# A two-layer RWKV-7 and latent-attention trunk: token lerps as a scaled sum on ScalarE and VectorE instead of GpSimd differences, and a new order at the start

## The chip, the core and the metric

The kernel runs on one core of one Trainium2 chip. The metric is device time in microseconds for one execution. The core has TensorE (PE: matmul, with its weight loads shown apart as PEld), VectorE (DVE), ScalarE (ACT), GpSimd (POOL) and SyncE (SP), which here only issues transfers. Each engine takes its instructions in the order of its own queue and waits at semaphores for the others.

## What is computed

The input, 512 tokens of width 1024 with 16 learned tokens put ahead of them (528 in all), goes through two layers. The first is an RWKV-7 mixer, the second a latent attention; the changed code is at the start of the first:

```python
h = concatenate([meta, x])
u = rms_norm(h, norm_pre[0])
u_prev = pad(u, one row ahead)[:-1]
dx = u_prev - u
# for each of six weights c = r, k, v, g, w_lo, a_lo, with a vector mu_c of 1024 numbers
h_c = (u + mu_c * dx) @ W_c
w = -softplus(-(w0 + tanh(w_lo) @ w2)) - 0.5
a = sigmoid(a0 + a_lo @ a2)
# then a recurrence over the tokens for 32 heads, its output normed, times silu(g), times W_out
```

Here `u + mu_c * dx` is the "lerp" of a token and the one before it.

## The kernel before

**Layout.** A token tile is [128 channels x 528 tokens], so the 1024 channels are 8 tiles, k = 0 to 7. The tile of the normed token has one column more, a zero ahead: columns 1 to 528 are u, columns 0 to 527 are the token before. To keep float32 precision at the speed of a faster form, each operand of a big product is split in a rounded high part and a rest, and three products are summed (high by high, high by rest, rest by high). So each token tile is split by ScalarE (a copy, the high part) and VectorE (a difference, the rest), and each 128x512 piece of weights by ScalarE (copy) and GpSimd (difference).

**Stages of the first layer.** `norm` reads the 8 tiles, squares them on ScalarE, sums them over the channels (on TensorE, by a product with a matrix of ones), and makes u. `lerps` runs in two lanes (even and odd k), each with one buffer (`sq` or `inv`) for the lerp; it takes the six weights in the order c = 2 (v), 4, 5 (the two small ones, "lora"), 3 (g, stored in DRAM), 1 (k), 0 (r). So there are 48 lerps, 8 for each c. `gemm` makes the projections, 48 matmuls each: v0 to v2 together, then v3, v4, lora 4, v5, lora 5, v6 to v13, k0, r0, k1, r1, v14, v15, k2, r2 and so on, and last 16 of g. `decays` makes w and a for all 16 head pairs (128 matmuls) when the lerps are done. `prepare`, `within`, `sides`, `invert`, `recur` and `finish` do the recurrence pair by pair; `prepare` begins behind the last of the decays. The projections of later pairs and of g fill TensorE meanwhile, and what is left of them runs behind the last pair.

**What sets the order.** All stages are generators that yield small steps. `Flow.run` picks among them the one that could start first, by a table of costs, and so writes out the queue of every engine beforehand; on the chip only the semaphores count. `flow.warm` names an f16 product into an unused part of a PSUM bank, which `Flow.cold` puts in where TensorE would idle, as a fill. The event "norm" is raised when the norm's factor (`ysq`) is made. `yield flow.until("norm")` so moves a step back in the written order; it is no wait on the chip.

**Names in the trace.** Tiles are reused, so the names say little at the start: u for k = 0 to 7 lies in SV, KBt, MR, KB, ALR, ALR, ALR, vx; the raw tokens, and then dx, lie beside them (the last in M). The split lerps of c = 2 lie in the other halves of SV, KBt, MR and so on; those of the others in `x`, and in `k` and `r` for c = 3. `w` is a split weight, `wraw` (or `X`) the raw one. All recorded instructions have one line, L322 (L327 after the change), that of the recorder.

Of the kernel before, what the change touches and what calls it, by code (L numbers as in the profile page):

```python
# [5 lines left out]
F32 = mybir.dt.float32  # L6
F32R = mybir.dt.float32r
F16 = mybir.dt.float16
AF = mybir.ActivationFunctionType
ALU = mybir.AluOpType  # L10
# [4 lines left out]
T = 528  # L15
# [46 lines left out]
class K:  # L62
# [14 lines left out]
    def consts(self):  # L77
        nc = self.nc
        cp = self.cp = self.pool("consts", 1)
        self.par = cp.tile([128, Par.n], F32, name="par")  # L80
        self.ones, self.ident, self.center = (cp.tile([128, 128], F32, name=n) for n in ("ones", "ident", "center"))
        self.bones = cp.tile([128, 128], F32, name="bones")
        self.omka = cp.tile([128, NP], F32, name="omka")
        nc.gpsimd.memset(self.ones, 1.0)
        scalars = cp.tile([128, 3], F32, name="scalars")
        for i, (name, x) in enumerate((("eps_gn", GN_EPS), ("one", 1.0), ("eps_rms", RMS_EPS))):
            t = scalars[:, i : i + 1]
            setattr(self, name, t)
            nc.gpsimd.memset(t, x)

    def load(self, nc):

        nc.sync.dma_start(self.par, self.a["par"])
        yield
        nc.sync.dma_start(self.ident, self.a["cst"][:, 0:128])
        yield
        nc.sync.dma_start(self.center, self.a["cst"][:, 128:256])
        yield
        o, w = Par.off["k_a"]
        nc.vector.tensor_scalar(self.omka, self.par[:, o : o + w], -1.0, 1.0, ALU.mult, ALU.add)  # L100
        nc.vector.tensor_copy(self.bones, self.center)
        nc.vector.scalar_tensor_tensor(self.center, self.center, -1.0 / 64, self.ident, ALU.mult, ALU.add)
        yield
# [354 lines left out]
class Layer0:  # L458
# [19 lines left out]
    def tl(self, bufs, shape, tag, dt=F32):  # L478
        return self.l[bufs].tile(list(shape), dt, name=self.g.nm(tag), tag=tag)
# [26 lines left out]
    def tables(self):  # L506

        nc = self.nc
        yield self.flow.until("x")
        yield from self.g.load(nc)  # L510
        for i in range(2):
            raw = self.tl(1, (128, 320), ("Mb", "Qb")[i])
            nc.sync.dma_start(raw, self.g.a["cst"][:, 256 + 320 * i : 576 + 320 * i])
            yield
            nc.vector.tensor_copy(self.masks[:, 5 * i : 5 * i + 5], raw.rearrange("p (m t) -> p m t", t=64))
            yield
        m = self.masks.rearrange("p m t -> p (m t)")

        self.bank, self.outs = self.psum("pc", 512, 1), self.psum("py", 512, 1)
        self.flow.cut[self.bank.tensor.name] = 128  # L520
        self.flow.cut[self.outs.tensor.name] = 256
        self.flow.warm = self.bank[:, 256:512], m[:, 0:128], m[:, 128:384]

    def norm(self):

# [6 lines left out]
        for k in range(KT):  # L532
# [4 lines left out]
            if k == KT - 1:  # L537
                nc.event("x")
            yield
        self.dx = xs  # L540
        self.place()
        part = [tl(1, (128, T), "P"), tl(1, (128, T), "gx")]
        nc.scalar.preload_act_table_set(EXP_LN)
        for k in range(KT):
            if k < 2:
                nc.scalar.activation(part[k], xs[k], AF.Square)
            else:
                sq = tl(1, (128, T), ("c", "a")[k % 2])
                nc.scalar.activation(sq, xs[k], AF.Square)
                yield  # L550
                (nc.gpsimd if k in (3, 5) else nc.vector).tensor_tensor(part[k % 2], part[k % 2], sq, ALU.add)
            yield
        out = self.two()
        for i in range(2):
            for (q, v), (b, e) in zip(out, HALVES):
                nc.tensor.matmul(v, g.ones, part[i][:, b:e], start=(i == 0), stop=(i == 1))
            yield
        rstd = tl(1, (128, T), "ysq")
        for (q, v), (b, e) in zip(out, HALVES):
# [4 lines left out]
        nc.event("norm")  # L564
        for k in range(KT):
            u = self.u[k]
            nc.vector.scalar_tensor_tensor(u[:, 1:], self.dx[k], g.p("norm_pre0", k), rstd, ALU.mult, ALU.mult)
            yield
            nc.gpsimd.tensor_tensor(self.dx[k], u[:, :T], u[:, 1:], ALU.subtract)
            nc.event(("u", k))  # L570
            yield
        self.places += [self.spare, tl(1, (128, T), "ysq", F32R)]
# [14 lines left out]
    def lerps(self, lane):  # L587
# [5 lines left out]
        for c in (2, 4, 5, 3, 1, 0):  # L593
            if c in late:
                yield self.flow.until(late[c])
            for k in range(lane, KT, 2):
                yield self.flow.until("u" if k == KT - 1 else ("u", k))
                xc = tl(1, (128, T), ("sq", "inv")[lane])
                nc.vector.scalar_tensor_tensor(xc, self.dx[k], g.p(f"mu{c}", k), self.u[k][:, 1:], ALU.mult, ALU.add)
                yield  # L600
                if c == 3:
                    h, l = tl(2, (128, T), "k", F32R), tl(2, (128, T), "r", F32R)
# [118 lines left out]
    def decays(self, lane):  # L721
# [9 lines left out]
        def read(j):  # L731
            t = tl(1, (128, 256), names[0])
            nc.sync.dma_start(t, g.a["w2a2"][j])
            return t

        raw = read(lane)
        yield flow.until(("lora", 4), ("lora", 5), ("lerps", 0), ("lerps", 1))
        for j in range(lane, NP, 2):
# [525 lines left out]
    def stages(self):  # L1264
        self.later = []
        self.x = {c: {} for c in range(6)}
        self.units()
        return [self.finish(), self.recur(1), self.recur(0), self.sides(), self.invert(0), self.invert(1), self.within(), self.prepare(), self.tables(), self.norm(),
                self.lerps(0), self.lerps(1), self.decays(0), self.decays(1)], [self.gate(), self.regate(), self.reload()]


WRAW = 2
# [928 lines left out]
```

## Time and profile before

| | us |
|---|---|
| median of 3 runs | 1610.45 |
| lowest and highest | 1608.45, 1613.81 |
| the profiled execution, its own time | 1609.79 |
| its span in the trace | 1608.0 |
| TensorE busy | 1463.8 |
| VectorE busy | 1034.9 |
| ScalarE busy | 942.4 |
| GpSimd busy | 733.9 |

The profiled execution lies 0.66 us below the median. 1.8 us of its time lie outside the span of the trace. A busy time of TensorE holds the latency of its products, which overlap, so a busy engine is not one at its peak.

### The profile page before, as it was taken

To read this page: it belongs to the slowest core of one execution; us is meant where nothing else is said; L and a number is where in the kernel's file an instruction comes from. 1 tells how busy PE (TensorE), PEld (TensorE's weight loads), DVE (VectorE), ACT (ScalarE), POOL (GpSimd) and SP (SyncE) were. 2 spreads that over 40 slices of the span, in tenths; PEclk is the share of its full clock that TensorE was granted. 3 is DMA by queue.
4 is the path that set the end of the run, shared out by engine and by line. 5 is a ranking of instruction groups with operands and counts; after the bars stand their busy time and mean duration, and the time that the engine had idled before them with its cause. 6 is when DMAs were issued, how large, how long until landed. Compare 5 with 4: busy or idle time off the path is not lost. (4 is left out here: it accounts for less than half of the span.)

```text
span 1608.0 us, 33360 instructions
## 1 busy us (share of the span) xinstructions
PE 1463.8 (91%) x12404; PEld 1301.2 (81%) x12404; DVE 1034.9 (64%) x2304; ACT 942.4 (59%) x2467; POOL 733.9 (46%) x877
## 2 busy tenths in 40 slices
PE   3899988899998998999998999999999999989997
PEld 3898877888887887888887899998778778877786
DVE  7995688787788877778777333035476666656503
ACT  3556655767766667677777674445555545544532
POOL 4453555444544435444445565745523222322654
PEclk7999999999999999999999999999999999999998
DMA  3456622122122122112422257533211111211332
GB/s 113 133 188 223 205 81 74 43 68 68 55 64 66 61 68 68 49 61 88 143 74 82 69 164 253 171 101 93 82 46 48 53 46 54 53 51 45 112 94 84
DMA packets 84690, 148.49 MB, mean 92 GB/s; under 512 B 9392, under 2 KB 18480, under 8 KB 84528
## 3 DMA queue, kind: packets, MB, share of 16 engines
q1 hardware_dynamic: 84528, 146.37, 28.9%
q8 instruction: 97, 1.59, 0.4%
q14 instruction: 65, 0.53, 0.1%
HBM read 112.87 MB, written 33.46 MB: 91 GB/s over the span
## 5 line engine op out<-in xcount | busy, mean ns | idle before, releaser
L322 POOL TENSOR_TENSOR w<-wraw,w 128x512 fp32r<-128x512 f32 (+1 forms) x278 | 371.6, 1343 | 478.8 <-ACT w L322 448.6
L322 PE MATMUL pg<-x,w 128*128 128x264 f32 x2064 | 337.5, 299 | 7.7 <-ACT k L322 3.2
L322 PEld LDWEIGHTS pg<-x,w 128*128 128x128 f32 x2064 | 272.7, 189 | 13.7 <-ACT k L322 5.7
L322 ACT ACTIVATE w<-wraw 128x512 fp32r<-128x512 f32 (+1 forms) x278 | 170.2, 615 | 135.7 <-DMA wraw<-wo 58.5
L322 POOL COPY Sd<-SV 64x64 f32<-64x64 f32 x256 | 73.1, 286 | 187.9 <-DVE SV L322 180.3
L322 PE MATMUL pb<-u,w 128*128 128x512 f32 x384 | 106.2, 405 | 11.9 <-DVE sg L322 11.9
L322 PE MATMUL pg<-lat,w 128*128 128x512 f32 (+1 forms) x480 | 108.5, 367 | 4.9 <-DVE q L322 3.1
L322 PEld LDWEIGHTS pg<-lat,w 128*128 128x128 f32 x480 | 80.6, 197 | 17.4 <-DVE q L322 3.5
L322 PEld LDWEIGHTS pb<-u,w 128*128 128x128 f32 x384 | 68.4, 190 | 25.8 <-DVE sg L322 14.2
L322 PE MATMUL pg<-O,w 128*128 128x512 f32 x336 | 79.1, 395 | 3.2 <-ACT acc L322 1.5
L322 PEld LDWEIGHTS pg<-O,w 128*128 128x128 f32 x336 | 62.9, 188 | 19.1 <-ACT acc L322 1.9
L322 DVE SCALAR_TENSOR_TENSOR SV<-Sd,PC,pc 64x64 f32<-64x64 f32 x224 | 59.8, 279 | 22.3 <-PE pc L322 17.5
L322 PE MATMUL pc<-xs,Qd 128*128 128x64 f32 x288 | 54.4, 286 | 20.4 <-ACT xs L322 19.0
L322 PEld LDWEIGHTS <-Mb 128*128 128x128 f16 x1152 | 59.0, 98 | 16.4 <-issue 6.4
L322 POOL TENSOR_TENSOR Lb<-M,Mh 64x256 f16<-64x256 f32 (+1 forms) x64 | 50.4, 787 | 42.8 <-ACT Mh L322 38.8
L322 PEld LDWEIGHTS pc<-xs,Qd 128*128 128x128 f32 x288 | 41.4, 189 | 34.3 <-ACT xs L322 29.8
L322 PE MATMUL pc<-SV,KBt 128*128 128x128 f32 x256 | 54.2, 312 | 9.5 <-DVE SV L322 7.6
L322 DVE SCALAR_TENSOR_TENSOR sg<-sg,par,rs 128x264 f32<-128x264 f32 x32 | 16.0, 532 | 71.9 <-ACT rs L322 71.9
L322 DVE TENSOR_TENSOR Xs<-pw,masks 128x128 f16<-128x128 f32 (+1 forms) x160 | 47.7, 301 | 21.4 <-PE pw L322 9.6
L322 DVE COPY SV<-pc 64x64 f32<-64x64 f32 x176 | 36.3, 225 | 38.4 <-ACT SV L322 32.7
L322 PE MATMUL pw<-Tm,Mb 128*128 128x32 f16 (+1 forms) x864 | 54.7, 180 | 4.8 <-ACT Tm L322 3.8
L322 PE MATMUL pc<-SV,ALR 128*128 128x128 f32 x288 | 57.2, 286 | 1.1 <-ACT xs L322 0.5
(375 smaller groups left out, 3906.7 us busy)
## 6 DMA issues: line engine op xcount, KB each, us to landing
wraw<-wr SPq DMA_DIRECT2D x120, 256.0 KB, 2.9
wraw<-wo SPq DMA_DIRECT2D x64, 256.0 KB, 2.7
wraw<-wi SPq DMA_DIRECT2D x46, 256.0 KB, 2.7
d_v<-gx SPq DMA_DIRECT2D x16, 264.0 KB, 3.0
d_c<-o SPq DMA_DIRECT2D x16, 264.0 KB, 2.4
c<-d_c SPq DMA_DIRECT2D x16, 264.0 KB, 3.0
a<-d_a SPq DMA_DIRECT2D x16, 264.0 KB, 3.1
vx<-d_v SPq DMA_DIRECT2D x16, 264.0 KB, 2.9
```

What stands on the lines that cost most here:

```text
L322: getattr(eng, method)(*args, **kw)
```

## The change

Six edits, all at the start of the first layer:

1. GpSimd's eight differences `dx = u_prev - u` are gone. A lerp was one VectorE instruction, `mu * dx + u`. It is now one ScalarE instruction, `(1 - mu) * u` (a copy with a scale for each channel, from the new small table `ommu`), and one VectorE instruction, `mu * u_prev +` that. Both write the lane's one buffer.
2. The norm's squares have a tile each and are summed by pairs (four VectorE sums, where there were four on VectorE and two on GpSimd), and each pair is multiplied by the ones on TensorE (eight products of 264 columns, where there were four).
3. `flow.warm` is set before anything is loaded, on the matrix of ones read as f16, instead of behind the load of the masks. Fill can stand from the first us.
4. The loads of `ident`, `center` and the masks, and the first of `w2a2`, are written behind the event "norm"; those of weights come ahead of them.
5. `omka`, `bones` and `center` move with their loads.
6. In the list of stages the lerps stand ahead of `norm`, so that they win where two steps could start at about the same time.

```diff
--- before.py
+++ after.py
+        self.ommu = cp.tile([128, 6 * KT], F32, name="ommu")
...
-    def load(self, nc):
+    def load(self, nc, flow):
 
         nc.sync.dma_start(self.par, self.a["par"])
         yield
+        o = Par.off["mu0"][0]
+        nc.vector.tensor_scalar(self.ommu, self.par[:, o : o + 6 * KT], -1.0, 1.0, ALU.mult, ALU.add)
+        yield
+        yield flow.until("norm")
         nc.sync.dma_start(self.ident, self.a["cst"][:, 0:128])
...
     def tables(self):
 
         nc = self.nc
+
+        self.bank, self.outs = self.psum("pc", 512, 1), self.psum("py", 512, 1)
+        self.flow.cut[self.bank.tensor.name] = 128
+        self.flow.cut[self.outs.tensor.name] = 256
+        c = self.g.ones.bitcast(F16)
+        self.flow.warm = self.bank[:, 256:512], c[:, 0:128], c
         yield self.flow.until("x")
-        yield from self.g.load(nc)
+        yield from self.g.load(nc, self.flow)
...
-        self.flow.warm = self.bank[:, 256:512], m[:, 0:128], m[:, 128:384]
...
-        part = [tl(1, (128, T), "P"), tl(1, (128, T), "gx")]
         nc.scalar.preload_act_table_set(EXP_LN)
-        for k in range(KT):
-            if k < 2:
-                nc.scalar.activation(part[k], xs[k], AF.Square)
-            else:
-                sq = tl(1, (128, T), ("c", "a")[k % 2])
-                nc.scalar.activation(sq, xs[k], AF.Square)
+        out = self.two()
+        for i, tags in enumerate((("P", "gx"), ("c", "a"), ("sq", "inv"), ("k", "r"))):
+            part = [tl(2 if i == 3 else 1, (128, T), t) for t in tags]
+            for k in range(2):
+                nc.scalar.activation(part[k], xs[2 * i + k], AF.Square)
                 yield
-                (nc.gpsimd if k in (3, 5) else nc.vector).tensor_tensor(part[k % 2], part[k % 2], sq, ALU.add)
-            yield
-        out = self.two()
-        for i in range(2):
+            nc.vector.tensor_tensor(part[0], part[0], part[1], ALU.add)
+            yield
             for (q, v), (b, e) in zip(out, HALVES):
-                nc.tensor.matmul(v, g.ones, part[i][:, b:e], start=(i == 0), stop=(i == 1))
+                nc.tensor.matmul(v, g.ones, part[0][:, b:e], start=(i == 0), stop=(i == 3))
             yield
...
-            nc.gpsimd.tensor_tensor(self.dx[k], u[:, :T], u[:, 1:], ALU.subtract)
             nc.event(("u", k))
...
                 xc = tl(1, (128, T), ("sq", "inv")[lane])
-                nc.vector.scalar_tensor_tensor(xc, self.dx[k], g.p(f"mu{c}", k), self.u[k][:, 1:], ALU.mult, ALU.add)
+                n = KT * c + k
+                nc.scalar.activation(xc, self.u[k][:, 1:], AF.Copy, scale=g.ommu[:, n : n + 1])
+                yield
+                nc.vector.scalar_tensor_tensor(xc, self.u[k][:, :T], g.p(f"mu{c}", k), xc, ALU.mult, ALU.add)
                 yield
...
+        yield flow.until("norm")
         raw = read(lane)
...
-        return [..., self.prepare(), self.tables(), self.norm(),
-                self.lerps(0), self.lerps(1), self.decays(0), self.decays(1)], [...]
+        return [..., self.prepare(), self.tables(), self.lerps(0), self.lerps(1), self.norm(),
+                self.decays(0), self.decays(1)], [...]
```

Three places show how the written order moves.

VectorE's queue, from the first normed token on, before (SV, KBt, MR, KB, ALR with `par` and `ysq` are the norm's; `sq` and `inv` the lerps; SV_275 the rest of the first split):

```order
L322 SCALAR_TENSOR_TENSOR SV_246<-SV_246,par,ysq_337 128x528
L322 SCALAR_TENSOR_TENSOR KBt_247<-KBt_247,par,ysq_337 128x528
L322 SCALAR_TENSOR_TENSOR MR_248<-MR_248,par,ysq_337 128x528
L322 SCALAR_TENSOR_TENSOR sq_359<-SV_246,par 128x528
L322 SCALAR_TENSOR_TENSOR KB_249<-KB_249,par,ysq_337 128x528
L322 SCALAR_TENSOR_TENSOR ALR_250<-ALR_250,par,ysq_337 128x528
L322 TENSOR_TENSOR SV_275<-sq_359,SV_275 128x528
L322 SCALAR_TENSOR_TENSOR ALR_250<-ALR_251,par,ysq_337 128x528
L322 SCALAR_TENSOR_TENSOR sq_371<-MR_248,par 128x528
L322 SCALAR_TENSOR_TENSOR inv_362<-KBt_247,par 128x528
```

The same place after the change:

```order
L327 SCALAR_TENSOR_TENSOR SV_249<-SV_249,par,ysq_346 128x528
L327 SCALAR_TENSOR_TENSOR KBt_250<-KBt_250,par,ysq_346 128x528
L327 SCALAR_TENSOR_TENSOR MR_251<-MR_251,par,ysq_346 128x528
L327 COPY bones<-center 128x128
L327 SCALAR_TENSOR_TENSOR center<-center,ident 128x128
L327 SCALAR_TENSOR_TENSOR sq_364<-SV_249,par,sq_364 128x528
L327 SCALAR_TENSOR_TENSOR inv_370<-KBt_250,par,inv_370 128x528
L327 SCALAR_TENSOR_TENSOR KB_252<-KB_252,par,ysq_346 128x528
L327 CAST masks<-Mb_376 128x320
L327 CAST masks<-Qb_384 128x320
L327 TENSOR_TENSOR SV_290<-sq_364,SV_290 128x528
L327 TENSOR_TENSOR KBt_291<-inv_370,KBt_291 128x528
```

Before, the constants' work stood ahead of the first normed token, and the rest of the first lerp came behind five of the norm's instructions. Now `bones` and `center` and the masks' two casts stand among the first lerps, two lerps go side by side, and the first rest comes behind four of the norm's.

ScalarE's queue where the lerps of c = 4 begin, before (`x` is the high part of a lerp, `w` that of a weight, `gx` the copy of a projection):

```order
L322 ACTIVATE x_497<-inv_488 128x528
L322 ACTIVATE w_513<-X_183_353 128x512
L322 ACTIVATE x_520<-sq_508 128x528
L322 ACTIVATE x_550<-sq_542 128x528
L322 ACTIVATE x_559<-inv_532 128x528
L322 ACTIVATE x_578<-sq_569 128x528
L322 ACTIVATE x_593<-inv_587 128x528
L322 ACTIVATE w_610<-wraw_500 128x512
L322 ACTIVATE x_613<-sq_602 128x528
```

And after, at the same lerps:

```order
L327 ACTIVATE sq_508<-SV_249,ommu 128x528
L327 ACTIVATE inv_520<-KBt_250,ommu 128x528
L327 ACTIVATE x_532<-sq_508 128x528
L327 ACTIVATE x_543<-inv_520 128x528
L327 ACTIVATE sq_556<-MR_251,ommu 128x528
L327 ACTIVATE inv_566<-KB_252,ommu 128x528
L327 ACTIVATE x_574<-sq_556 128x528
L327 ACTIVATE x_584<-inv_566 128x528
L327 ACTIVATE sq_594<-ALR_253,ommu 128x528
L327 ACTIVATE inv_604<-ALR_253,ommu 128x528
L327 ACTIVATE w_611<-wraw_497 128x512
```

Each pair of lerps now has four instructions in ScalarE's queue, the two scalings and then the two high parts; the weights' splits stand between them.

TensorE's queue at the first pair's preparation (`sq,bones` is its first product, `w` with SV, KBt or x is the projections), before:

```order
L322 MATMUL pw_2460<-SV_275,w_2330 128x264 x2
L322 MATMUL pw_2460<-SV_275,w_2331 128x264
L322 MATMUL pw_2444<-sq_2404,bones 128x264
L322 MATMUL pw_2445<-sq_2404,bones 128x264
L322 MATMUL pw_2461<-SV_275,w_2330 128x264 x2
L322 MATMUL pw_2461<-SV_275,w_2331 128x264
L322 MATMUL pw_2460<-KBt_276,w_2330 128x264 x2
L322 MATMUL pw_2460<-KBt_276,w_2331 128x264
```

And after:

```order
L327 MATMUL pg_2578<-x_1539,w_2535 128x264
L327 MATMUL pg_2578<-x_1540,w_2535 128x264
L327 MATMUL pg_2578<-x_1539,w_2536 128x264
L327 MATMUL pw_2727<-sq_2686,bones 128x264
L327 MATMUL pw_2728<-sq_2686,bones 128x264
L327 LDWEIGHTS ones
L327 MATMUL pc_247<-ones 128x256
```

Before, 963 matmuls of the projections stand ahead of the pair's first product, and v14's go on behind it. After, 1104 of them stand ahead of it, up to the whole of k2, and fill follows. The decays' first product stands behind 654 projection matmuls before the change, and behind 804 after it.

## Rows read from the trace of the kernel before

**Rows 1.** The page: busy time by engine, and TensorE's busy tenths in 40 slices.

```profile
PE 1463.8 (91%) x12404; PEld 1301.2 (81%) x12404; DVE 1034.9 (64%) x2304; ACT 942.4 (59%) x2467; POOL 733.9 (46%) x877
...
PE   3899988899998998999998999999999999989997
```

**Rows 2.** All engines in two later stretches: busy us (count), clock, transfers, GB/s.

```profile
209.30:500.00 290.70, 264.80 (x2970) 234.56 (x2966) 237.06 (x623) 196.46 (x602) 134.18 (x214) 0.99 0.19 62
...
883.00:1000.00 117.00, 113.74 (x935) 110.04 (x934) 42.53 (x83) 76.69 (x169) 66.96 (x68) 1.00 0.50 164
```

**Rows 3.** Timeline to 26 us: start, duration (us), engine, instruction, idle before.

```profile
11.09 0.64 ACT L322 ACTIVATE a<-M 128x528 f32<-128x528 f32 x1 [0.84 <-POOL gx L322]
...
11.85 2.10 PE L322 MATMUL pw<-P,ones 128*128 128x264 f32 x4 [11.85 <-DVE bones L322]
...
14.26 0.63 ACT L322 ACTIVATE w<-X 128x512 fp32r<-128x512 f32 x1 [1.25 <-DMA X<-wr]
...
16.94 0.77 DVE L322 SCALAR_TENSOR_TENSOR SV<-SV,par,ysq 128x528 f32<-128x528 f32 x1 [0.30 <-ACT ysq L322]
...
17.78 1.52 POOL L322 TENSOR_TENSOR SV<-SV 128x528 f32<-128x528 f32 x1 [1.33 <-DVE SV L322]
18.30 1.57 DVE L322 SCALAR_TENSOR_TENSOR MR<-MR,par,ysq 128x528 f32<-128x528 f32 x1
...
19.79 1.56 DVE L322 SCALAR_TENSOR_TENSOR sq<-SV,par 128x528 f32<-128x528 f32 x1
...
23.45 1.57 DVE L322 TENSOR_TENSOR SV<-sq,SV 128x528 fp32r<-128x528 f32 x1
...
25.07 1.47 PE L322 MATMUL pg<-SV,w 128*128 128x264 f32 x5 [2.40 <-DVE SV L322]
```

**Rows 4.** TensorE by stretches, columns as in rows 2.

```profile
12.00:14.00 2.00, 2.00 (x5) 1.00 0.73 252
20.00:22.00 2.00, 0.00 (x0) 0.50 0.00 0
34.00:36.00 2.00, 2.00 (x10) 0.50 0.00 0
```

**Rows 5.** The timeline from 41 to 55 us.

```profile
41.60 0.70 DVE L322 TENSOR_TENSOR ysq<-inv,Y 128x528 fp32r<-128x528 f32 x1
...
42.87 0.40 PE L322 MATMUL pg<-ALR,w 128*128 128x264 f32 x2
...
54.03 0.28 PE L322 MATMUL pw<-Y,w 128*128 128x264 f32 x1
```

**Rows 6.** All engines in three stretches, columns as in rows 2.

```profile
42.34:128.10 85.76, 76.07 (x589) 73.53 (x587) 80.64 (x82) 48.54 (x96) 41.63 (x28) 0.98 0.49 163
128.10:187.60 59.50, 57.83 (x429) 55.68 (x429) 32.07 (x35) 43.41 (x105) 19.86 (x19) 0.94 0.72 245
187.60:209.30 21.70, 17.58 (x151) 16.58 (x149) 18.45 (x18) 7.74 (x17) 17.33 (x22) 0.94 0.36 122
```

**Rows 7.** Groups, 42 to 128 us: count, busy us, mean ns, idle before.

```profile
L322 DVE TENSOR_TENSOR x<-inv,x 128x528 fp32r<-128x528 f32 x16 | 15.1, 943 | 2.9 <-ACT x L322 2.8
...
L322 ACT ACTIVATE x<-inv 128x528 fp32r<-128x528 f32 x16 | 10.3, 646 | 16.3 <-DVE inv L322 16.2
...
L322 POOL TENSOR_TENSOR w<-wraw,w 128x512 fp32r<-128x512 f32 x18 | 28.2, 1573 | 37.4 <-ACT w L322 27.3 <-PE pw L322 9.8
```

**Rows 8.** The timeline of the first pair's preparation.

```profile
187.61 0.72 ACT L322 ACTIVATE sq<-k,par 128x528 f32<-128x528 f32 x1
...
188.58 1.05 PE L322 MATMUL pw<-sq,bones 128*128 128x264 f32 x4
...
198.95 3.58 DVE L322 TENSOR_TENSOR KB<-sq,c 64x576 f32<-64x576 f32 x2
...
202.54 1.52 DVE L322 TENSOR_TENSOR KB<-inv,a 64x576 f32<-64x576 f32 x2
...
209.50 1.51 PE L322 MATMUL pw<-ALR,KB 64*128 64x128 f32 x16
```

More of the change, by code (lines that the diff above doesn't have):

```diff
@@ L516, in tables @@
             yield
[L517 to L521, printed above, removed]
-        self.flow.warm = self.bank[:, 256:512], m[:, 0:128], m[:, 128:384]
     def norm(self):
@@ L539, in norm @@
             yield
-        self.dx = xs
         self.place()
-        part = [tl(1, (128, T), "P"), tl(1, (128, T), "gx")]
         nc.scalar.preload_act_table_set(EXP_LN)
-        for k in range(KT):
-            if k < 2:
-                nc.scalar.activation(part[k], xs[k], AF.Square)
-            else:
-                sq = tl(1, (128, T), ("c", "a")[k % 2])
-                nc.scalar.activation(sq, xs[k], AF.Square)
+        out = self.two()
[3 more added lines that the diff above has]
+                nc.scalar.activation(part[k], xs[2 * i + k], AF.Square)
                 yield
-                (nc.gpsimd if k in (3, 5) else nc.vector).tensor_tensor(part[k % 2], part[k % 2], sq, ALU.add)
+            nc.vector.tensor_tensor(part[0], part[0], part[1], ALU.add)
             yield
-        out = self.two()
-        for i in range(2):
             for (q, v), (b, e) in zip(out, HALVES):
-                nc.tensor.matmul(v, g.ones, part[i][:, b:e], start=(i == 0), stop=(i == 1))
+                nc.tensor.matmul(v, g.ones, part[0][:, b:e], start=(i == 0), stop=(i == 3))
             yield
@@ L566, in norm @@
             u = self.u[k]
-            nc.vector.scalar_tensor_tensor(u[:, 1:], self.dx[k], g.p("norm_pre0", k), rstd, ALU.mult, ALU.mult)
-            yield
-            nc.gpsimd.tensor_tensor(self.dx[k], u[:, :T], u[:, 1:], ALU.subtract)
+            nc.vector.scalar_tensor_tensor(u[:, 1:], xs[k], g.p("norm_pre0", k), rstd, ALU.mult, ALU.mult)
             nc.event(("u", k))
@@ L1267, in stages @@
         self.units()
-        return [self.finish(), self.recur(1), self.recur(0), self.sides(), self.invert(0), self.invert(1), self.within(), self.prepare(), self.tables(), self.norm(),
-                self.lerps(0), self.lerps(1), self.decays(0), self.decays(1)], [self.gate(), self.regate(), self.reload()]
+        return [self.finish(), self.recur(1), self.recur(0), self.sides(), self.invert(0), self.invert(1), self.within(), self.prepare(), self.tables(), self.lerps(0), self.lerps(1), self.norm(),
+                self.decays(0), self.decays(1)], [self.gate(), self.regate(), self.reload()]
 WRAW = 2
```

## Prediction

> **What bounds the kernel now.** I read the page first. TensorE is busy for 91% of the span, no other engine above 64%, and its tenths are 8 or 9 in nearly every slice except the first, which has 3 [rows 1]. Two stretches tell what a saved microsecond at the start is worth. From the first pair's products on, TensorE is busy for 264.8 of 290.7 us; behind the last pair, from 883 us on, it does what is left of the projections for 113.7 of 117.0 us [rows 2]. So a pair of heads takes its time, the projections fill its gaps, and what did not fit runs behind at full rate. A change at the start counts in two ways: by when the first pair starts, and by how many projection matmuls are done by then.
>
> Then I read the start itself. TensorE's first projection at full supply begins at 25.07 us [rows 3]. Ahead of it is a chain: the squares (the last waited 0.84 us for a GpSimd sum), the ones' products (2.10 us for four), the splits of weights on ScalarE (the third waited for its transfer until 14.26), the factor, the first normed token at 16.94, then GpSimd's 1.52 us difference, the first lerp at 19.79 and its rest at 23.45. VectorE takes 1.57 us where the same instruction takes 0.77 without GpSimd [rows 3]. The last rest of c = 2 ends at 42.30, and TensorE ends the first three projections at 54.31 [rows 5]. From there to 128.1 VectorE is busy for 80.6 of 85.8 us, TensorE for 76.1, ScalarE for only 48.5 [rows 6]. TensorE does the projections at 76.07 / 589 = 0.129 us each there. Then come the decays, and at 187.6 the first pair's preparation, whose first product stands at 209.50 [rows 6, 8].
>
> **The change part by part.**
>
> *The norm.* Without the wait for GpSimd the last square can start at 10.25 instead of 11.09. The eight ones' products stand behind squares that come earlier, and only the last pair's lie behind the last square: a sum of 0.70 and about 2.0 of products, done near 13.7, beside ScalarE's three splits. If the third split's transfer lands as before, nothing is gained; if it lands in time, the split starts near 12.1. Five small loads no longer stand ahead of it, so I take 12.6, and with the 2.68 us from there to the first normed token, 15.2 instead of 16.94 [rows 3].
>
> *The first fill.* Fourteen fill products stand at the very start. The granted clock reads 1.00 (2.4 GHz) at 12 to 14 us, when nothing had run before, and 0.50 (1.2 GHz) from 20 us, with TensorE idle since about 16 [rows 4]; four products of the ones took 2.10 us there, four of the same size at 188 us took 1.05 [rows 3, 8]. So the first ones ran at half speed whatever the column says. Between the fill and the last ones' products TensorE has little to do, so I count no gain. The Trainium skill (TensorE: Matmul & The Clock Gate, What's actually happening) says that a hardware monitor sets the clock by how busy the array was recently, so fill that ends microseconds ahead would have been in vain. By that rule the change's "from the first us" is worth nothing; the two durations agree with it, the granted column in rows 4 does not.
>
> *The first eight lerps.* No GpSimd difference stands between token and lerp, and VectorE is not stretched. Its list from 15.2 to the first rest is four norms, two lerps (0.77 each), `bones` and `center` (0.5), two casts (1.3) and the rest (0.70): 22.3, against 25.02. That the constants now stand here costs 1.8; at nothing they were hidden before, while TensorE and ScalarE made the factor. The whole list is 16 x 0.77 + 8 x 0.70 + 1.8 = 19.8, so 35.0 against 42.30. ScalarE's 16 scalings and copies (0.72 and 0.65) lie beside it. TensorE has 72 products for k = 0 to 3, 25 of them at half clock (0.2 us, ten in 2 us in rows 4) and 47 at 0.129: 22.3 + 5.0 + 6.1 = 33.4. Behind k = 3 come the splits of three new pieces of weights, as before, and k = 4 to 7 took 54.31 - 42.87 = 11.4 [rows 5]. So the first three projections end at 44.8 instead of 54.31: 9.5 us gained here, with 6 to 11.5 as bounds (no gain from the norm; VectorE at the rate of its starts).
>
> *The other forty lerps.* Here the change costs. ScalarE gets 40 scalings of 0.72 [rows 8] in a stretch where it has 37 us to spare, so the sum fits; the wait is what counts. Before, a lane's chain was lerp, copy, rest. Now it is scaling, lerp, copy, rest on one buffer: 0.72 + 0.77 + 0.65 + 0.70 and four hand-overs of about 0.05, so 3.0 us for two lerps, one in each lane, of which VectorE itself needs 2.94. GpSimd's splits still stretch VectorE, a rest from 0.70 to 0.943 in the mean [rows 7]: four instructions, 1.0. ScalarE's other work (splits, copies of projections) is 48.54 - 40 x 0.646 = 22.7 us, 1.14 for two lerps. If it is hidden, a lerp takes 2.0 us; if all of it delays the chain, 2.57; before it took 85.8 / 40 = 2.14. Halfway, 2.3, ends them at 35.0 + 92 = 127; the ends are 115 and 138. What is queued behind a late scaling is the split of weights, for which GpSimd and then TensorE wait. TensorE itself reaches the decays behind 804 matmuls instead of 654: 44.8 + 660 x 0.129 = 130. The later of the two counts: 130 against 128.1, with 140 where the lerps set it.
>
> *The decays and the first pair.* 428 matmuls up to the preparation instead of 437, at 59.5 / 437 = 0.136: 188.3 against 187.6. In the first pair's preparation the projections are used up (k2 waits for this very pair), so no weights are split, and VectorE's products take 1.52 instead of 3.58 [rows 8]: 2.1 off 21.9, hence 208.1 against 209.50, so -1.4. TensorE idles or runs fill meanwhile.
>
> *Work done ahead.* Counted along TensorE's written order at the ends of pairs 2, 4 ... 14, the new order has 24, -9, 36, 18, 27, 18 and 30 projection matmuls more behind it, 21 in the mean, at 0.129: 2.7 us. Of the pairs' own work it has 17 more in the mean, at 290.7 / 2970 = 0.098: 1.6 us.
>
> **Sum.** -1.4 - 2.7 - 1.6 = -5.7. Against the profiled execution's 1609.79 that is 1604.1, and with the 0.66 by which it lies below the median 1604.8. So of the 9.5 us gained by 45 us, lerps and decays give back some two fifths. I say 1605.
>
> **Rivals.**
>
> 1. *ScalarE keeps up.* The lerps are hidden, fill keeps the clock up, and the decays come at 126 (TensorE's 660 at 0.123). Then 4 us more: 1601, and with the casts hidden too 1598. ScalarE's 37 us of idle time speak for it [rows 6]; that each copy waits for a VectorE that is stretched speaks against it.
> 2. *All is given back.* The lerps end at 136, the first pair starts 5 us late and the work ahead pays for it: 1610. Bounds of 133 and 139 give 1607 to 1613. For it: four hand-overs on one buffer, where two buffers kept VectorE at 94%.
> 3. *Slower: ScalarE's queue starves TensorE.* If the splits of weights stand behind scalings that wait for the rest before, a lerp takes 2.75 us and more, the lerps end at 145 or later, and TensorE waits in the lora projections and in k0. The decays come 17 us late; the work ahead pays 4 and the quiet preparation 2: +11, 1621. It decides from 2.55 us for a lerp on.
> 4. *The change does not do what it says.* The fill at the start and the sums by pairs change nothing if the third split's transfer lands as late as before; that costs 1.7 of the 9.5 and lies in the range.
>
> **How the numbers follow.** The forecast, 1601 to 1609, has 0.48, rival 1 has 0.17, rival 2 0.22, rival 3 0.13. A measurement of this kernel tells some 0.3%, 4.8 us, from no change. Of the forecast, 0.28 lies beyond that and 0.20 within; rival 1 is faster; rival 2 is the same but for 0.02 on either side; rival 3 is slower: faster 0.47, same 0.38, slower 0.15. The range from 1595 to 1615 leaves out most of rival 3 and the best end of rival 1.
>
> **What would show it.** The first normed token near 15.2; the first projection at full supply near 22.3; the first three projections done near 45; no VectorE instruction over 1 us before 32; 2.3 us for a lerp and the decays from 130; the preparation near 188; its first product near 208. I am wrong if ScalarE's waits for VectorE and TensorE's for ScalarE or GpSimd between 45 and 130 come to more than 10 us, or if the pairs run at another pace than before, since the new order differs there too and I take its pace as unchanged.

## The result and the profile after

The changed kernel is slower: 1619.37 us in the median of 7 runs (1617.43 to 1623.40), against 1609.56 for 7 runs of the kernel before (1603.13 to 1613.81). The ratio is 1.0068, with a 95% interval from 1.0046 to 1.0089. I had said 1605, in a range that ends at 1615. The profiled execution took 1622.68 us, its span 1620.9; that is 12.9 us more than the span of the kernel before, where the medians differ by 9.8.

The page of the changed kernel, busy time and tenths, to set beside [rows 1]:

```profile
PE 1476.8 (91%) x12472; PEld 1310.9 (81%) x12472; DVE 1019.3 (63%) x2305; ACT 970.7 (60%) x2515; POOL 716.4 (44%) x867
...
PE   6999779999999999888888999999999999989997
...
PEclk8999999999999999998999999999999999999999
```

The first slices are fuller. TensorE is busy 13 us longer in all, with 68 instructions more, and about halfway there is a row of 8s that was not there before. The start itself, in the timeline (start, duration, engine, instruction, idle before), against [rows 3, 5, 8]:

```profile
1.00 3.17 PE L327 MATMUL pc<-ones 128*128 128x256 f16 x14 [1.00 <-POOL ones L85]
5.69 2.13 PE L327 MATMUL pw<-P,ones 128*128 128x264 f32 x4 [1.52 <-DVE P L327]
...
10.65 1.05 PE L327 MATMUL pw<-k,ones 128*128 128x264 f32 x4
...
11.34 0.63 ACT L327 ACTIVATE w<-X 128x512 fp32r<-128x512 f32 x1
...
13.42 1.62 DVE L327 SCALAR_TENSOR_TENSOR SV<-SV,par,ysq 128x528 f32<-128x528 f32 x1 [2.87 <-ACT ysq L327]
...
20.75 1.47 PE L327 MATMUL pg<-SV,w 128*128 128x264 f32 x5 [1.90 <-DVE SV L327]
...
43.41 0.29 PE L327 MATMUL pw<-Y,w 128*128 128x264 f32 x1
...
131.16 0.28 PE L327 MATMUL pw<-Qd,Q 128*128 128x264 f32 x1
...
188.69 0.72 ACT L327 ACTIVATE sq<-k,par 128x528 f32<-128x528 f32 x1
...
189.46 0.71 PE L327 MATMUL pw<-sq,bones 128*128 128x264 f32 x2 [1.86 <-ACT sq L327]
...
207.43 1.48 PE L327 MATMUL pw<-ALR,KB 64*128 64x128 f32 x15 [4.00 <-DVE ALR L327]
```

The start came sooner than I forecast or at most 1.2 us later: the first three projections end at 43.7, the first pair's product stands at 207.43, and 1104 projection matmuls lie behind it where the kernel before had done 1068 at 209.50. That is 2.1 us, and 36 matmuls at 0.129: 6.7 us ahead. My sum had 5.7 in all, of which -1.4 and -2.7 are these two; its other 1.6 was for the pairs' own work.

So the loss must come later. I put TensorE's last `pc<-xs,Qd` of a pair as its end and cut both traces there. Columns of this view: stretch, its length, busy us and count for PE, PEld, DVE, ACT and POOL, granted clock, share of the DMA engines, GB/s. The kernel before: to the end of pair 9, of pair 16, to the first layer's last product, and the first two together:

```profile
209.50:640.80 431.30, 391.65 (x4375) 348.57 (x4374) 346.70 (x923) 292.36 (x894) 199.29 (x321) 0.99 0.20 64
640.80:929.90 289.10, 266.31 (x2889) 238.08 (x2889) 206.06 (x590) 204.09 (x622) 142.49 (x226) 1.00 0.25 81
929.90:1026.98 97.08, 96.26 (x781) 95.50 (x782) 25.50 (x25) 58.00 (x108) 60.70 (x47) 1.00 0.65 207
209.50:929.90 720.40, 657.96 (x7262) 586.64 (x7261) 552.76 (x1512) 496.45 (x1516) 341.78 (x546) 0.99 0.22 71
```

The changed kernel, the same four:

```profile
207.43:631.00 423.57, 388.99 (x4351) 345.19 (x4351) 337.50 (x920) 288.01 (x889) 195.89 (x317) 0.98 0.19 62
631.00:953.40 322.40, 286.50 (x2994) 257.20 (x2994) 219.66 (x599) 214.44 (x642) 151.01 (x235) 0.96 0.24 81
953.40:1040.72 87.32, 84.83 (x683) 83.34 (x683) 19.61 (x21) 48.36 (x91) 50.30 (x39) 1.00 0.65 209
207.43:953.40 745.97, 675.49 (x7343) 602.39 (x7343) 557.16 (x1517) 502.45 (x1530) 346.90 (x551) 0.97 0.21 70
```

At the end of pair 9 the changed kernel is 9.8 us ahead, at that of pair 16 it is 23.5 us behind. Some of that is projections done earlier: 2880 by the end of pair 16, against 2781. To take them out I subtract 0.129 us for each projection matmul within the stretch, and call the rest the net length of the pairs. Before it is 720.40 - 1713 x 0.129 = 499.4, after it is 745.97 - 1776 x 0.129 = 516.9: 17.5 us more for the same work, since without projections and fills TensorE has 5541 instructions there before and 5540 after. By the same count pairs 1 to 9 are 4 us shorter than before, and pairs 10 to 16 some 22 us longer. With the start's -6.7, +3.0 in the first layer's rest (87.32 - 673 x 0.129 against 97.08 - 772 x 0.129) and -0.9 in the second layer, that is the +12.9 us of the two spans.

No line of the diff touches these pairs. What differs is the order in which they were written, and what waits there. TensorE's waits in the changed kernel, from pair 10 to 16 (us in total, times, longest):

```profile
PE pc L327 <- ACT xs L327: 11.9, 18, 2.1
PE pc L327 <- DVE SV L327: 6.7, 14, 1.2
PE pw L327 <- DVE Xs L327: 3.1, 4, 1.8
PE pg L327 <- DMA x<-d_xg: 2.0, 2, 1.2
```

In the kernel before, in its own stretch of those pairs:

```profile
PE pc L322 <- ACT xs L322: 8.1, 24, 0.8
PE pc L322 <- DVE SV L322: 3.9, 9, 0.9
```

The recurrence's own steps (`pc` waits for `xs` and `SV`) wait longer at a time, up to 2.1 us instead of 0.9. Behind the longest wait the granted clock is half, as the changed kernel's windows show (columns as above):

```profile
723.60:730.40 6.80, 4.58 (x43) 4.16 (x43) 5.62 (x13) 4.63 (x15) 4.89 (x6) 1.00 0.00 0
730.40:737.20 6.80, 6.22 (x43) 5.95 (x44) 3.60 (x11) 3.89 (x14) 1.41 (x2) 0.50 0.13 41
737.20:744.00 6.80, 6.53 (x100) 6.06 (x99) 3.65 (x15) 5.35 (x21) 1.01 (x6) 1.00 0.13 41
```

TensorE waited from 728.7 to 730.77 and was busy for 4.58 of 6.8 us; then it ran at 0.50 (1.2 GHz) for as long, busy for 6.22 us, and at 1.00 (2.4 GHz) again behind that. The same happens at 761, 792 and 812 us. In all the clock is half for 23.9 us between 640 and 953, and for none between 640 and 930 before, where the view above reads 1.00. The Trainium skill (TensorE: Matmul & The Clock Gate, What's actually happening) says that a monitor sets the clock by how busy the array has been of late; these rows agree.

So the 17.5 us by size: TensorE idles 745.97 - 675.49 = 70.5 us between the first product and the end of pair 16 against 62.4, +8; over the same length it is busy at half clock for 34.9 us against 10.8 (the trace's instructions laid over its clock), of which half is lost, +12; what is left, -2.6, is not explained. This is an account, with work at half clock taken at twice its time; no run here takes the two terms apart.

### The profile page after: what moved, and what is told of

Read it like the earlier page. It is cut to its first block, busy times and chain, and to the rows that moved or that the text cites. A ratio compares the mean times of both kernels' runs of the same rounds, so it can differ in the third digit from the quotient of the medians.

```text
span 1620.9 us, 33517 instructions
## 1 busy us (share of the span) xinstructions
PE 1476.8 (91%) x12472; PEld 1310.9 (81%) x12472; DVE 1019.3 (63%) x2305; ACT 970.7 (60%) x2515; POOL 716.4 (44%) x867
## 5 line engine op out<-in xcount | busy, mean ns | idle before, releaser
L327 PE MATMUL pg<-x,w 128*128 128x264 f32 x2112 | 353.6, 303 | 10.9 <-ACT gx L327 3.3
L327 PEld LDWEIGHTS pg<-x,w 128*128 128x128 f32 x2112 | 286.0, 193 | 15.3 <-ACT gx L327 3.8
L327 DVE TENSOR_TENSOR Xs<-pw,masks 128x128 f16<-128x128 f32 (+1 forms) x160 | 47.0, 301 | 24.1 <-PE pw L327 11.3
L327 ACT ACTIVATE Tm<-pw 128x128 f16<-128x128 f32 (+1 forms) x160 | 44.6, 285 | 28.6 <-PE pw L327 26.2
L327 PEld LDWEIGHTS pc<-SV,KBt 128*128 128x128 f32 x256 | 37.4, 195 | 27.1 <-DVE SV L327 14.2
```

What stands on the lines that cost most here:

```text
L327: getattr(eng, method)(*args, **kw)
```

## The experiments

My theory after the result: **the start gained what was forecast, and the order in which the pairs are written, which the planner changes whenever anything ahead of them changes, loses more.** The rival: **the new start itself makes the pairs slower**, because it leaves less projection work to fill their gaps and brings other arrivals. A smaller question is what the half clock costs.

**The two orders exchanged.** Both orders were recorded while the kernels were built. The one kernel's start is kept up to the end of the decays, and from there every engine follows the other's order, less what is already done:

```diff
+            if not follow and "decays2" in self.events:
+                follow = True
...
+            if follow:
+                for n, x in enumerate(left):
...
+                    if self.start(s[1], j) is not None:
+                        break
+                left.pop(n)
...
+                best = (0, x[0], j)
```

`left` is the other kernel's recorded order.

> The changed kernel up to the decays; from there on every engine follows the order written for the kernel before, its few stand-in matmuls included, without what is already done. Theory (the order in which the pairs are written makes the loss): the start keeps its 2 us at the first product ALR,KB and the 9.8 us of the end of pair 9, the loss of pairs 10 to 16 is gone, no stretch of half clock between 640 and 930 us, and the time is 1601 to 1607 us, under the kernel before. Rival (the changed start itself, which leaves the pairs less projection work and other arrivals, makes them slower in any order): TensorE's waits of pairs 10 to 16 come again, 1615 us or more.

It took 1608.85 us, 0.9991 of the kernel before (0.9976 to 1.0007), above the theory's range and below the rival's. Its row from the first product to the end of pair 16, and that of the first pair's end:

```profile
206.96:931.00 724.04, 658.18 (x7225) 585.64 (x7225) 551.73 (x1513) 494.92 (x1513) 341.05 (x545) 0.98 0.22 70
206.96:290.60 83.64, 71.35 (x735) 60.08 (x736) 68.74 (x172) 49.03 (x141) 39.13 (x55) 0.91 0.19 59
```

The clock around the first product, and the wait ahead of that product:

```profile
191.30:211.80 20.50, 6.55 (x57) 5.07 (x57) 14.77 (x24) 4.21 (x8) 8.77 (x16) 0.50 0.07 25
...
206.96 1.44 PE L516 MATMUL pw<-ALR,KB 64*128 64x128 f32 x10 [10.95 <-DVE ALR L516]
```

The loss is gone with the order: 1.0068 - 0.9991 = 0.0077, some 12 us better than the changed kernel. But the forecast gain isn't there. It is lost in the first pair: from the first product to that pair's end it takes 83.64 us, where the kernel before takes 81.90 with 36 matmuls more; from there to the end of pair 16 the two are 1.9 us apart. Two things differ there. The 36 matmuls that were done ahead are missing as filler in the first pair. And the order of before has none of the 27 fills that the changed kernel runs ahead of its first product, so TensorE idles for 10.95 us there, and the clock is half from 191 to 212 us. How much each of them costs isn't shown. So the rival has a part: an order that was written for a later start doesn't use an earlier one.

> The kernel before up to the decays; from there on every engine follows the order written for the changed kernel, what that had done earlier first. Theory (the order makes the loss): the waits and the four stretches of half clock of pairs 10 to 16 appear although no instruction is edited, and the time is 1618 to 1630 us. Rival (the start makes it): the time of the kernel before, 1605 to 1613 us.

1638.81 us, ratio 1.0176 (1.0155 to 1.0196), more than the theory's range allowed. The profiled span, 1639.0, is 31.0 us longer than that of the kernel before. 15.3 of these lie ahead of the first product, which stands at 224.85 because what the other start had done earlier is caught up there; in return 36 projection matmuls more are done by then, 4.6 us; and the pairs' net length is 520.9 against 499.4, 21.5 us more. No instruction of the change is in this kernel, and it has the changed kernel's loss. The four stretches of half clock come again, 17.9 us later than in the changed kernel, as the first product comes 17.4 us later:

```profile
748.30:755.10 6.80, 6.59 (x50) 6.20 (x51) 3.65 (x13) 3.62 (x12) 1.44 (x2) 0.50 0.10 36
779.00:789.20 10.20, 9.33 (x43) 7.27 (x44) 7.44 (x19) 1.07 (x4) 2.46 (x7) 0.50 0.03 13
809.70:819.90 10.20, 10.19 (x77) 9.33 (x78) 1.77 (x6) 4.56 (x15) 2.79 (x6) 0.50 1.02 382
830.20:837.00 6.80, 6.47 (x43) 5.63 (x43) 5.32 (x17) 1.24 (x3) 0.84 (x4) 0.50 0.12 39
```

**Other orders of the same pairs.** From the decays on, the planner's constants are moved a little. Nothing else changes; each kernel issues the same work, but for the fills. The edit of redraw b:

```diff
             best, known = None, len(self.events)
+            if "decays2" in self.events:
+                self.SLACK = 0.09; self.DEFER = 0.085
```

> The changed kernel; one constant of the order's planner (the head start that a stage further down its list needs to go first) is 0.12 us in place of 0.10 from the decays on, so that the same instructions of the pairs are written in another order. Theory (the loss belongs to one written order, not to the start): the time differs from the changed kernel's by several us, most likely below it, 1600 to 1615 us. Rival (the start makes it): 1617 to 1623 us whatever the order.

> The changed kernel; from the decays on the planner's constants are 0.105 (head start of a later stage), 0.075 (delay of a projection's step) and 0.4 (advance of one when TensorE runs short), so that the same instructions of the pairs are written in another order, one that the planner's own clock ends 20 us earlier than the changed kernel's. Theory (the written order decides, and the start costs nothing): another time again, some us under the changed kernel, 1600 to 1615 us. Rival (the start makes the pairs slower): 1617 us or more, as in the changed kernel and in the order with 0.12.

> The kernel before, with nothing of the change; one constant of the planner is 0.08 in place of 0.10 from the decays on. Theory (the order of the kernel before is an unusually good one, and whatever makes the planner write another loses it): 1620 to 1645 us although the start is the old one. Rival (orders from the old start are all about as good, and only the new start leads to slow ones): 1605 to 1613 us.

> The changed kernel with 0.09 and 0.085 for the first two of the planner's constants from the decays on, a third order of the same pairs (16 us earlier than the changed kernel's by the planner's own clock). Theory: another time again, 1603 to 1620 us, with stretches of half clock in other places than 730 to 816 us. Rival: 1617 to 1623 us, half clock in the same places.

> The kernel before with 0.09 in place of 0.10 for the delay of a projection's step from the decays on: a second other order of its pairs, by the planner's own clock 2 us behind the kernel before, where the first redraw was 33 us behind. If the planner's clock tells good orders from bad ones: 1605 to 1618 us. If it doesn't, and other orders are mostly slow: 1620 to 1655 us.

> The changed kernel with 0.08 for the delay of a projection's step from the decays on: a fourth other order of its pairs, 13 us ahead of the changed kernel's by the planner's own clock. Theory (the start keeps its gain wherever the order is good): 1598 to 1612 us. Rival: 1617 us or more.

Every kernel's stretch from its first product `ALR,KB` to the end of pair 16 (idle is length less PE busy; the net length takes 0.129 off for each projection in it; "at half" is the time that PE is busy at half clock; fills are counted from 250 us on):

| kernel | first product, us (matmuls done) | length | idle | clock | at half | projections in it | net length | fills | ratio to before (95%) |
|---|---|---|---|---|---|---|---|---|---|
| before | 209.50 (1068) | 720.40 | 62.4 | 0.99 | 10.8 | 1713 | 499.4 | 1 | 1 |
| changed | 207.43 (1104) | 745.97 | 70.5 | 0.97 | 34.9 | 1776 | 516.9 | 14 | 1.0068 (1.0046, 1.0089) |
| changed, 0.12 | 205.81 (1104) | 778.79 | 83.4 | 0.96 | 53.2 | 1776 | 549.7 | 31 | 1.0345 (1.0322, 1.0369) |
| changed, redraw a | 207.43 (1104) | 730.57 | 63.6 | 0.97 | 39.2 | 1707 | 510.4 | 1 | 0.9995 (0.9978, 1.0013) |
| changed, redraw b | 208.88 (1104) | 731.62 | 64.4 | 1.00 | 0 | 1821 | 496.7 | 1 | 0.9941 (0.9925, 0.9957) |
| changed, redraw c | 206.40 (1104) | 735.60 | 59.9 | 0.99 | 18.8 | 1824 | 500.3 | 0 | 0.9964 (0.9951, 0.9978) |
| before, 0.08 | 209.20 (1068) | 785.40 | 83.8 | 0.96 | 54.3 | 1905 | 539.7 | 25 | 1.0277 (1.0256, 1.0298) |
| before, redraw 2 | 208.06 (1068) | 725.94 | 62.0 | 1.00 | 7.0 | 1785 | 495.6 | 0 | 1.0014 (0.9999, 1.0028) |

The rows of the worst redraw of either start and of the best, each from its own windows. The changed kernel with 0.12:

```profile
205.81:984.60 778.79, 695.42 (x7353) 613.35 (x7354) 572.67 (x1517) 499.25 (x1530) 338.60 (x551) 0.96 0.21 67
```

The kernel before with 0.08:

```profile
209.20:994.60 785.40, 701.64 (x7473) 627.79 (x7470) 574.88 (x1521) 511.69 (x1549) 359.81 (x562) 0.96 0.22 71
```

The changed kernel in redraw b:

```profile
208.88:940.50 731.62, 667.23 (x7373) 595.76 (x7373) 569.22 (x1519) 505.56 (x1537) 349.32 (x554) 1.00 0.23 73
```

The same work takes 1599 to 1664 us behind the changed start, and 1609 to 1652 behind the old one. The first products of all eight lie within 4 us, the net lengths spread over 54. So the order decides, by some nine times what my sum had for the whole change; the kernel before has the best of its own three orders, and the changed kernel the fourth best of its five. The account of waits and half clock also fits the redraws roughly. Against the kernel before, more idle time and half of the longer time at half clock give +42 for 0.12 (net length +50), +15 for redraw a (+11), -3 for b (-3), +2 for c (+1), +43 for 0.08 (+40) and -2 for redraw 2 (-4). By this account both terms count: redraw a loses nearly all of its 11 us by the clock, with 1.2 us more idle time.

My expectation for 0.12 (better) was wrong, the others came out inside their ranges but for redraw b, which was better than its range, and that for 0.08, which was worse. The planner's own clock, as those texts give it (none for 0.12), tells the good from the bad but not among the good: the order it puts 33 us behind was 44 us slower on the chip, the one it puts 2 us behind as good as before; of the three that it puts 13, 16 and 20 us ahead of the changed kernel's, all three were faster, but the one with 16 the most.

The fills tell much the same, and stand in the written order. They are what the planner puts in where it finds TensorE idle for long. The changed kernel, grouped by tile and form from 250 us on (count, busy us, mean ns, idle before):

```profile
L327 PE MATMUL pc<-ones 128*128 128x256 f16 x14 | 3.7, 370 | 0.8 <-DVE SV L327 0.7 <-ACT xs L327 0.2
```

And the changed kernel with 0.12:

```profile
L327 PE MATMUL pc<-ones 128*128 128x256 f16 x31 | 7.9, 299 | 3.4 <-DVE SV L327 2.9 <-ACT SV L327 0.4
```

With 0 or 1 fill behind 250 us the orders above give 1599 to 1613, with 14 they give 1619, with 25 and 31 they give 1652 and 1664. It is a sign and no law: redraw a has one fill and a mean clock of 0.97, and the kernel with the old lerps, below, has one and took 1626.

**The start's worth in a good order.** The order of redraw b, written out, behind the old start; it is followed from the first pair's products on. Against the edit of the exchange:

```diff
-            if not follow and "decays2" in self.events:
+            if not follow and ("products", 0) in self.events:
```

> The kernel before up to the first pair's products; from there on every engine follows the order that redraw b (1599 us) was written in, the 36 projection matmuls that its start had done more coming first. Theory (in an order that keeps TensorE busy and at full clock the changed start is worth its 2 us and its 36 matmuls, 6.7 us): 1604 to 1608 us, no half clock between the first product and the end of pair 16. Rival (only the order matters, the start is worth nothing, as in the order of the kernel before): 1597 to 1601 us.

1607.32 us, ratio 0.9987 (0.9977 to 0.9996), against 0.9941 with the changed start and the same order: 0.0046 x 1610 = 7.4 us, and the intervals don't meet. That is the theory's time, though two stretches of half clock remain (6.8 us). Its rows, to the end of pair 16, to the first layer's last product and behind it:

```profile
208.70:944.00 735.30, 675.69 (x7441) 605.01 (x7437) 566.50 (x1518) 508.22 (x1541) 352.67 (x556) 1.00 0.23 74
944.00:1027.03 83.03, 79.39 (x637) 78.10 (x638) 16.15 (x19) 44.16 (x83) 45.88 (x36) 1.00 0.64 202
1027.03:1604.40 577.37, 538.18 (x3126) 457.08 (x3124) 291.39 (x591) 273.09 (x603) 234.10 (x194) 0.99 0.25 72
```

The last two of redraw b:

```profile
940.50:1021.66 81.16, 78.78 (x637) 77.71 (x638) 15.13 (x19) 44.03 (x83) 46.10 (x36) 1.00 0.66 208
1021.66:1596.40 574.74, 536.28 (x3126) 456.03 (x3124) 290.92 (x591) 273.15 (x603) 233.66 (x194) 0.99 0.25 72
```

Its net length is 735.30 - 1857 x 0.129 = 495.7, as good as the 496.7 of redraw b, and its first product stands at 208.70, that of redraw b at 208.88; what it lacks is the 36 matmuls. By the end of pair 16 it is 944.00 - 940.50 = 3.5 us behind. The spans, 1604.4 and 1596.4, differ by 8.0; the other 4.5 us come behind the pairs, 1.9 in the rest of the first layer and 2.6 in the second, with the same 637 and 3126 matmuls in both, and nothing here shows that the start makes them. So in this one order the kernel with the changed start is 7.4 us faster, and the rows trace 3.5 of that to the work done ahead; my forecast of 5.7 lies between.

**The clock.** The question is whether the half clock behind the waits costs time of its own. Stand-in products go ahead of the 25 matmuls of pairs 10 to 16 that waited over 0.5 us, in the changed kernel's own order:

```diff
         for method, args, kw in op.calls:
+            if op.eng == "tensor":
+                for _ in range(FILLS.get(self.count, 0)):
+                    eng.matmul(*self.warm, start=True, stop=True)
+                self.count += 1
             getattr(eng, method)(*args, **kw)
```

> The changed kernel in its own written order, with 4 to 16 stand-in matmuls (176 in all, of 256 columns each, into the same unread bank) put ahead of the 25 matmuls of pairs 10 to 16 that waited over 0.5 us. Theory (about half of the loss is TensorE's half clock behind those waits): the granted clock stays at full speed there, 24 us of half clock go, and 8 to 12 us come back: 1607 to 1612 us. Rival (the waits alone are the loss, and the clock falls in time that is lost anyway): 1617 to 1622 us.

1631.51 us, ratio 1.0136 (1.0120 to 1.0151). It fits neither side. The places were counted wrongly in this run, the fills stood ahead of other matmuls, and the waits stayed: it only shows that 176 fills in the wrong places cost 12 us.

> The changed kernel in its own written order, with the 176 stand-in matmuls of the earlier run, now each group right ahead of the matmul that waited (in that run they stood ahead of other matmuls, and the waits stayed). A group takes about as long as the wait that it stands in (0.127 us a matmul). Theory (about 12 us of the loss is the half clock that follows those waits): half clock between 640 and 955 us falls from 24 us to under 10, TensorE's idle time there from 36 us to under 20, and the time is 1608 to 1614 us. Rival (the clock falls in time that is lost anyway): 1617 to 1623 us.

1622.66 us, ratio 1.0083 (1.0066 to 1.0100), in the rival's range and no better than the changed kernel. Its windows, pairs 10 to 16:

```profile
631.10:955.20 324.10, 296.89 (x3170) 267.02 (x3170) 217.73 (x599) 214.37 (x642) 150.67 (x235) 0.99 0.25 80
```

And its group of fills there:

```profile
L333 PE MATMUL pc<-ones 128*128 128x256 f16 x176 | 24.1, 278 | 13.8 <-ACT xs L335 8.5 <-DVE SV L335 4.4 <-DVE xs L335 0.7
```

The clock did come back, from 0.96 to 0.99; half clock between 640 and 955 fell from 23.9 to 3.4 us. But the fills write the bank `pc` that ScalarE and VectorE were reading, and so they themselves waited for `xs` and `SV`, 13.8 us, and ran behind the wait, ahead of the product that was late. TensorE is busy with them for 24.1 us, and the time moved by nothing that can be told. So the fills' cost was paid back from somewhere, by the clock and by 9 us less of idle time, but the two can't be told apart here. A fill into a bank of its own was not tried. The 12 us for the half clock stay an accounting, not a thing shown by itself.

**The old lerps in the changed start.**

```diff
+            nc.gpsimd.tensor_tensor(xs[k], u[:, :T], u[:, 1:], ALU.subtract)
...
-                nc.scalar.activation(xc, self.u[k][:, 1:], AF.Copy, scale=g.ommu[:, n : n + 1])
-                yield
-                nc.vector.scalar_tensor_tensor(xc, self.u[k][:, :T], g.p(f"mu{c}", k), xc, ALU.mult, ALU.add)
+                nc.vector.scalar_tensor_tensor(xc, self.dx[k], g.p(f"mu{c}", k), self.u[k][:, 1:], ALU.mult, ALU.add)
```

> The changed kernel with the lerps of the kernel before (differences on GpSimd, one VectorE pass), the rest of the changed start kept; read up to the first product ALR,KB only, since the order behind it is written anew. If the norm sums by pairs bring the whole gain of the start: matmul 144 of the projections as in the changed kernel, at 43 to 45 us. If the lerps bring most of it: the first product at full supply 8.1 us behind the first normed token as before, at 21.5 us, and matmul 144 at 50 to 51 us; ALR,KB within 2 us of the changed kernel's 207.4 in either case, since the projections stop at the same wait.

A single run, 1625.67 us, read for the start only:

```profile
21.43 1.47 PE L327 MATMUL pg<-SV,w 128*128 128x264 f32 x5 [1.45 <-DVE SV L327]
...
46.15 0.28 PE L327 MATMUL pw<-Y,w 128*128 128x264 f32 x1
...
212.73 0.58 PE L327 MATMUL pw<-ALR,KB 64*128 64x128 f32 x2 [8.02 <-DVE ALR L327]
```

Matmul 144 stands at 46.15: of the 10.6 us between 54.03 and 43.41, the norm and the loads bring 7.9 and the lerps 2.7. The first product at full supply came as the second expectation had it (21.43 for 21.5), matmul 144 as neither had it, and the first pair's product was not within 2 us of 207.4 but 5.3 behind. So with the lerps on ScalarE 2.6 us more are gained on the way to the pairs; the order there is a new one too, so that this part may not be the lerps'.

## Why the prediction was wrong

The steps in its own order:

- **The norm: right in kind, larger than forecast.** The third split started at 11.34, not at 12.6, and the first normed token at 13.42, not at 15.2. Its transfer came in time, which I had left open.
- **The first fill: its own worth isn't shown.** Fourteen fills ended at 4.17, 0.23 us for one, where one of the 176 in the waits took 0.14; the first four products of the ones behind them still took 2.13 us, as long as the four of before [rows 3], the last four 1.05, with TensorE at work between. In the traces the clock's records begin only at 15.7 us (before) and at 10.1 us (after); ahead of them the column reads 1.00 without a record, so the 1.00 at 12 to 14 us in rows 4 is no measurement. The first of these products fit what I took from the Trainium skill's page (TensorE: Matmul & The Clock Gate, What's actually happening); the faster last ones, which I had counted at nothing, are part of the 1.8 us that the token came sooner than forecast.
- **The first eight lerps: right.** First product at full supply at 20.75 (forecast 22.3), first three projections done at 43.7 (44.8). VectorE was stretched over 1 us in only two instructions before 32 us, the first normed token (1.62) and one rest at 31.09 (1.47).
- **The other forty lerps: right.** Their copies run from 36.0 to 127.70, (127.7 - 36.0) / 39 = 2.35 us for one, forecast 2.3; the decays' first product stands at 131.16, forecast 130. Rivals 1 and 3 fell here. ScalarE's waits for VectorE between 45 and 130 come to some 14 us, above the 10 that I named as a sign of error; before they were over 33, so the sign was badly chosen.
- **The decays and the first pair: right in time, part of the reason wrong.** The preparation begins at 188.69 (188.3), its first product stands at 207.43 (208.1). It took 18.7 us, against 21.9 before: 3.15 less, where I had 2.1 from one couple of VectorE's products, `KB<-sq,c`. That couple took 2.54 instead of 3.58, not 1.52; the two products `ALR<-inv,P` and `ALR<-r,P` behind it took 0.75 and 0.74 instead of 1.72 and 1.88.
- **Work done ahead: right in count, wrong in what it is worth.** At the ends of pairs 2, 4 ... 14 the trace has just the counts that I took from the written order, 2.7 us in the mean; at the first product it was 36 matmuls, 4.6 us. With the order of before the start's lead is lost in the first pair; with redraw b it is kept.
- **The step that failed: "I take its pace as unchanged".** The pairs' pace, for which my sum had -1.6, cost 17.5 us net. I named it as what could make me wrong and gave it no price and no rival, though the written order lay before me: I counted projections and the pairs' own matmuls in it and not the fills, 14 behind 250 us where the kernel before has 1. Rival 2's time (1607 to 1613) was closer, and rival 3's time, 1621, was right for the wrong reason: nothing starves TensorE among the lerps.

What the runs show: the exchange and the redraws put the loss in the order of the pairs, not in the new instructions; the two kernels with one order are 7.4 us apart, 3.5 of them seen by the end of the pairs. What stays open: how the 17.5 us divide between waits and half clock, which of the planner's choices makes the waits, and what the 4.5 us behind the pairs are.

The version that beats both is the changed kernel in redraw b, 0.9941 of the kernel before (0.9925 to 0.9957), 1599.0 us; redraw c is also faster, 0.9964 (0.9951 to 0.9978).

## What to carry to other kernels

Where a planner or scheduler writes the order, an edit is two changes, its own and a new order for everything behind it; price the second too, from how far the time moves when the planner's constants are nudged with nothing else changed. Judge the edit with the order held (record it and follow it), and then draw a few orders for the changed kernel, since the constants were chosen for the old one. Before any run, read the written order for fills or other marks of an engine that the planner finds idle: 14 where there was 1 was the warning here.

## What the hardware showed that I had not expected

- Waits of 1.2 to 2.1 us were followed by 3.4 or 6.8 us at half clock, four times in the changed kernel between 640 and 953 us. The length of a wait alone doesn't tell: waits of 1.3 to 1.4 us at 649, 698 and 715 us were followed by none. Redraw b had no half clock between its first product and the end of pair 16 (clock 1.00 over 731.62 us), though its TensorE idled for 64.4 us there against 70.5 and waited up to 1.55 us at a time.
- TensorE's clock can be restored without gaining time: 176 stand-in products raised it from 0.96 to 0.99 and cost about what it gave.
- As written here, a stand-in product waits for the readers of the bank that it writes, 13.8 us for 176, though it writes an unread part of it.
